# Up-projections of a two-layer transformer: seven products of quarters in place of eight, and modulation vectors moved between engines

## The chip, the cores and the metric

One core of one Trainium2 chip runs the whole program. The metric is the device time of one execution in microseconds (us). The kernel before takes 1658.03 us (median of three runs, 1656.92 to 1659.02).

The engines named here are PE (TensorE, matrix products; PEld is its loading of weights), DVE (VectorE), ACT (ScalarE), POOL (GpSimd) and SP (SyncE, which issues the loads of weights). Each works through its own queue in order.

## The reference, cut to what matters

512 latent tokens (x) and 256 context tokens (ctx), 1024 features, two layers. Layer 1 returns no context, so its feed-forward part runs for x alone.

```python
D_MODEL = 1024; SEQ = 512; CTX_LEN = 256; DEPTH = 2; D_FF = 2816

def swiglu(h, w_up, w_down):
    a, b = jnp.split(h @ w_up, 2, axis=-1)
    return (jax.nn.silu(a) * b) @ w_down

def layer(x, ctx, mod_x, mod_c, ...):
    sh1, sc1, gt1, sh2, sc2, gt2 = jnp.split(mod_x[:, None, :], N_MOD, axis=-1)
    csh1, csc1, cgt1, csh2, csc2, cgt2 = jnp.split(mod_c, N_MOD, axis=-1)
    hx = rmsnorm(x, g1) * (1 + sc1) + sh1
    hc = rmsnorm(ctx, g1) * (1 + csc1) + csh1
    ...                       # input projection, three kinds of mixers
    x = x + gt1 * (jnp.concatenate([conv_x, attn_x, gla_x], axis=-1) @ w_out)
    x = x + gt2 * swiglu(rmsnorm(x, g2) * (1 + sc2) + sh2, w_up, w_down)
    if ctx_out:               # layer 0 only
        ctx = ctx + cgt1 * (jnp.concatenate([conv_c, attn_c, gla_c], axis=-1) @ w_out)
        ctx = ctx + cgt2 * swiglu(rmsnorm(ctx, g2) * (1 + csc2) + csh2, w_up, w_down)
    return x, ctx

def reference(...):
    for l in range(DEPTH):
        mod_x = jax.nn.silu(c) @ w_mod[l] + b_mod[l]        # w_mod[l]: 1024 x 6144
        mod_c = jax.nn.silu(c_ctx) @ w_mod[l] + b_mod[l]
        x, ctx = layer(x, ctx, mod_x, mod_c, ...)
    return rmsnorm(x, final_norm_g)
```

## The kernel before

**Streams and products.** All streams are kept feature-major: 128 features on the partitions, the 768 tokens (512 in layer 1's second half) along the free side, eight chunks of features. Every dense product is made in three passes of a 32-bit format that the matrix engine takes at full rate (`float32r`): a value is split into a high part (a copy into that format, on ACT) and a low part (the difference, on DVE), and the passes are high by high, high by low, low by high. `dense_pass` (L707) runs them for one column block of 128 output features: for each run of tokens (`XS`, 512, and `CS`, 256) eight chunks times three matmuls into a PSUM bank of the pool `main` (three banks), and then it calls the given function that takes the bank out. A second pool of five banks, `bank`, serves everything else.

**Weights.** A list `plan` holds every block of weights in the order of use. `w_advance` (L500) issues their loads on SP's queue into a ring of four buffers `raw` (`RAWS`, 512 KB each); a buffer is given back once its reader is done. It splits each block at its arrival into `whi` (ACT) and `wlo` (DVE), two buffers of each.

**Order.** `Plan` keeps a rough clock for each engine while the program is written; chains of work (mixers, norms) are Python generators that are stepped in between the matmuls when that clock says that their inputs are there (`spawn`, `poll`, `until`). The order of the queues is thus fixed when the program is built.

**Feed-forward part** (L1618 on). The 22 blocks of 128 hidden features are taken in `F_BLOCKS` (L30): six, six, six and four. For each hidden block f there are two dense passes, `a` and `b`; the bank of `a` goes through Silu on ACT, that of `b` is multiplied by it on DVE, and the result is split into two parts. At the end of each block of blocks come eight down-projections whose results are added to the streams (`residual`). The hidden blocks 0 and 1 are made by `Firsts` (L725), which follows the norm chunk by chunk of its features, so that PE works while the norm (`Normed.task`, L894) is still being made. The norm takes per chunk and run of tokens two DVE operations (scale; low part) and one of ACT (shift; high part). The norm's sums come with the output projection before it: `tail` (L1594) ends x's tokens first (`o2` with seven blocks for x, then the same for ctx), so that x's norm starts while PE makes ctx's products. In layer 1 the two runs are the halves of x, 256 tokens each.

**Modulation vectors.** `mod_todo` (L356) lists the column groups of `w_mod` that come beside other work, 512 columns each. Groups 4 to 8 of layer 0 are made on PE (`mod_step`, L626, four steps for each group; a step has four matmuls and reads one `raw` buffer of 512 KB; after the fourth the sums are turned by four transposes), beside layer 0's mixers. Groups 9 to 11 of layer 0 and all twelve of layer 1 are made on DVE (`mod_step_v`, L660): per step two rows of weights, each scaled and added to two accumulators (x, ctx) of 128x512, and after the fourth step a transpose and a sum for each accumulator. `mod_items` (L359) places these steps in the list of weights: one after most items of the input projection, two after each `o1` block, and one after each up- or down-projection of layer 0.

## Time and profile before

| | |
|---|---|
| median of three runs | 1658.03 us |
| span of the profiled execution | 1655.9 us |
| matmul instructions on PE | 11021 |
| DVE, ACT, POOL instructions | 2016, 1194, 58 |
| weights of the up-projections, loads of 512 KB | 80 |
| loads of `w_mod` of 512 KB | 92 |

The span is what the profiler saw of one execution, from its first to its last instruction; that execution's own time as a run is not recorded, and the median of the runs lies 2.1 us above the span. A row of the profile's groups reads: line, engine, operation, output from inputs, shapes, number; then busy time and the mean of one; then the idle time before them and what ended it. A name such as `main` or `raw` is the pool's buffer. In a timeline, a row starts with its start and its length in us.

### The profile page before, as it was taken

Reading aid. Unit: us, or ns where it says so; the run is one execution under the profiler, and the core shown is the slowest. Engines: PE = TensorE matmul, PEld = TensorE weight load, DVE = VectorE, ACT = ScalarE, POOL = GpSimd, SP = SyncE. Lnnn points to the kernel's source line nnn. Section 1 sums busy time; section 2 is a strip of 40 time slices with the busy share of each in tenths; the row PEclk is TensorE's granted clock in tenths of the full one; section 3 lists DMA queues with packets and bytes.
Section 4 is the critical chain, followed back from the end, with each engine's and each line's share of the span. In section 5 each row is a group of like instructions: output and inputs, shape, how many; then the busy total and the mean of one; then the engine's idle time right before and its main releaser. Section 6 shows DMA issues by size and latency. Waiting matters only on the chain.

```text
span 1655.9 us, 26996 instructions
## 1 busy us (share of the span) xinstructions
PE 1619.7 (98%) x11021; PEld 1371.7 (83%) x11026; DVE 1056.2 (64%) x2016; ACT 598.7 (36%) x1194; POOL 35.7 (2%) x58
## 2 busy tenths in 40 slices
PE   7999999999999999999999999998999999999998
PEld 5878778888888888888888888786889888888887
DVE  5687877669867766767752366879787533333336
ACT  4454544543422122112212235555474422223224
POOL 2000000000000000000000000000000000000002
PEclk9999999999999999999999999999999999999999
DMA  9830312244234544444442152201123233232322
GB/s 259 253 100 15 90 52 77 83 160 138 67 115 124 145 125 121 138 128 140 127 118 71 33 146 52 64 27 52 65 77 90 77 89 106 83 117 84 100 85 77
DMA packets 252540, 168.45 MB, mean 102 GB/s; under 512 B 29700, under 2 KB 232960, under 8 KB 252416
## 3 DMA queue, kind: packets, MB, share of 16 engines
q1 hardware_dynamic: 248832, 155.93, 32.8%
q0 software_dynamic: 1760, 5.47, 1.1%
q10 hardware_dynamic: 1824, 5.31, 0.9%
q8 instruction: 87, 1.43, 0.4%
q14 instruction: 37, 0.30, 0.1%
HBM read 159.35 MB, written 7.34 MB: 101 GB/s over the span
## 4 chain that ended last, share of the span: by engine, by line
PE 83%; DVE 8%; ACT 2%; issue 1%; DMA 0%; SPq 0%; DVEq 0%; ACTq 0%
PE main L136 69%; PE bank L136 11%; DVE act L185 3%; PE bank L140 3%; DVE t L185 1%; DVE t L213 1%; ACT t L152 1%; DVE mx L204 1%; DVE wlo L185 1%; ACT t L174 0%; DVE t L190 0%; DMA raw<-in_w_mod_dram 0%; DVE t L196 0%; DVE t L1140 0%; DVE act L196 0%
## 5 line engine op out<-in xcount | busy, mean ns | idle before, releaser
L136 PE MATMUL main<-act,whi 128*128 128x512 f32 (+1 forms) x4160 | 1131.1, 357 | 1.3 <-ACT act L152 1.3
L136 PEld LDWEIGHTS main<-act,whi 128*128 128x128 f32 x4160 | 731.8, 189 | 115.2 <-issue 9.1
L136 PE MATMUL main<-act,wlo 128*128 128x512 f32 (+1 forms) x2080 | 735.8, 354 | 1.7 <-DVE wlo L185 1.7
L136 PEld LDWEIGHTS main<-act,wlo 128*128 128x128 f32 x2080 | 393.0, 189 | 57.5 <-issue 2.7
L174 ACT CAST whi<-raw 128x1024 fp32r<-128x1024 f32 (+3 forms) x194 | 189.9, 979 | 486.7 <-PE main L136 455.6
L185 DVE TENSOR_TENSOR wlo<-raw,whi 128x1024 fp32r<-128x1024 f32 (+3 forms) x194 | 219.4, 1131 | 181.7 <-ACT whi L174 178.9
L196 DVE SCALAR_TENSOR_TENSOR t<-raw,cst,t 128x512 f32<-128x512 f32 x210 | 148.3, 746 | 40.9 <-DMA raw<-in_w_mod_dram 40.5
L196 DVE SCALAR_TENSOR_TENSOR act<-main,mods,act 128x512 f32<-128x512 f32 (+1 forms) x160 | 97.8, 614 | 96.5 <-PE main L136 95.4
L185 DVE TENSOR_TENSOR t<-main,t 128x256 f32<-128x256 f32 (+1 forms) x73 | 43.9, 601 | 110.2 <-PE main L136 106.8
L174 ACT CAST act<-t 128x512 fp32r<-128x512 f32 (+3 forms) x102 | 61.0, 599 | 124.8 <-DVE t L185 124.3
L152 ACT ACTIVATE t<-bank,nm 128x256 f32<-128x256 f32 (+1 forms) x144 | 69.7, 496 | 60.2 <-DVE nm L196 55.5
L136 PE MATMUL main<-act 128*128 128x256 f32 (+1 forms) x576 | 88.6, 311 | 0.0
L136 PEld LDWEIGHTS main<-act 128*128 128x128 f32 x576 | 79.9, 191 | 6.1 <-issue 0.3
L185 DVE TENSOR_TENSOR act<-t,act 128x512 fp32r<-128x512 f32 (+5 forms) x110 | 73.6, 672 | 12.7 <-ACT act L174 10.5
L136 PE MATMUL bank<-act,whi 128*128 128x256 f32 (+3 forms) x336 | 74.9, 298 | 0.0
L152 ACT ACTIVATE t<-main 128x512 f32<-128x512 f32 x69 | 36.2, 525 | 88.9 <-PE main L136 88.7
L136 PE MATMUL bank<-act 64*64 64x64 f32 (+2 forms) x608 | 62.7, 273 | 3.6 <-DVE act L185 3.4
L185 DVE TENSOR_TENSOR act<-act 128x768 f32<-128x768 f32 (+7 forms) x84 | 64.7, 782 | 1.3 <-ACT t L174 1.1
L204 DVE TENSOR_REDUCE mx<-bank 128x2 f32<-128x512 f32 (+2 forms) x104 | 56.2, 561 | 14.2 <-PE bank L136 13.7
L140 PE MATMUL bank<-tab,t 128*128 128x128 f32 (+1 forms) x396 | 56.4, 277 | 4.1 <-DVE nm L196 1.7
L136 PE MATMUL bank<-t,t 128*64 128x128 f32 (+1 forms) x720 | 58.0, 283 | 1.7 <-DVE t L200 1.5
L136 PEld LDWEIGHTS bank<-act 64*64 64x64 f32 (+1 forms) x608 | 47.8, 161 | 12.9 <-issue 5.4
(133 smaller groups left out, 1208.7 us busy)
## 6 DMA issues: line engine op xcount, KB each, us to landing
raw<-in_w_mod_dram SPq DMA_DIRECT2D x92, 512.0 KB, 4.2
raw<-in_w_up_dram SPq DMA_DIRECT2D x80, 512.0 KB, 3.9
raw<-in_w_down_dram SPq DMA_DIRECT2D x48, 384.0 KB, 3.4
raw<-in_w_in_dram SPq DMA_DIRECT2D x26, 512.0 KB, 4.0
raw<-in_w_in_dram SPq DMA_DIRECT2D x16, 256.0 KB, 3.8
raw<-in_w_out_dram SPq DMA_DIRECT2D x16, 256.0 KB, 2.9
raw<-in_w_out_dram SPq DMA_DIRECT2D x32, 128.0 KB, 3.0
raw<-in_w_up_dram SPq DMA_DIRECT2D x16, 256.0 KB, 4.3
```

Source lines behind the costliest of these rows:

```text
L136: self.pin("pe", self.nc.tensor.matmul(out, lhsT, rhs, start=start, stop=stop, **kw))
L140: self.pin("pe", self.nc.tensor.transpose(out, in_, ident))
L152: ins = self.pin("act", self.nc.scalar.activation(out, in_, func, **kw))
L174: self.pin("act", self.nc.scalar.copy(out, in_))
L185: self.pin(eng, self._v(eng).tensor_tensor(out, a, b, op))
L196: self.pin(eng, self._v(eng).scalar_tensor_tensor(out, a, s, b, op0, op1))
L204: self.pin("dve", self.nc.vector.tensor_reduce(out, in_, AX.X, op))
L213: self.pin("dve", self.nc.vector.copy_predicated(out, mask, data))
```

## The change

**Products.** Write the weights of a hidden block f as four quarters: `a1` is the block's `a` column half and `a2` its `b` half, split by features into k < 512 and k >= 512: a11, a12 (512 features by 128 columns each, from the `a` half), a21, a22. The normed stream is split by tokens into two halves and by features into two: b11, b21 for the first half of tokens, and the second half enters only through differences. Seven products of (four feature chunks) x (half the tokens: 384 in layer 0, 256 in layer 1) in Winograd's form of the scheme replace eight. Every one has 4 x 3 matmuls, so a hidden block takes 84 matmuls of 384 (256) columns; before, it took 48 of 512 columns, and in layer 0 another 48 of 256.

**Operands.** `Quartered` makes the seven operands of the norm (b11, b21, t1, b22, t2, t3, t4), each with its own high and low part: the sums for t1 to t4 on DVE, the high parts on ACT, the low parts on DVE. `Unit.make` makes the seven operands of the weights (a11, a12, a22, s1, s2, s3, s4; 128x512 each): two sums on POOL, two on DVE, seven high copies on ACT, seven low subtractions on DVE. The two `raw` buffers of the unit are used in place for these sums, and are given back after their last use.

**Banks.** p1, p6, p7 and p4 add up in one bank of `main` per unit (`v`), which is read out after each; p2 and p5/p3 use banks of `bank`.

**Order.** `run_units` writes the products of neighbouring units alternately, and operands three products ahead (`AHEAD`). At the start of a layer's feed-forward part the first two units go product by product side by side, p1 and p2 first, as the norm's operands come; `Firsts` is no longer used for the up-projections. Layer 0 takes five blocks (5, 5, 4, 4, 4) in place of four.

**Modulation.** Groups 9 to 11 of layer 0 are made on PE too, all of them before `o2` (four steps after each `o1` block). Layer 1's steps are still on DVE; for groups 4 and up, whose ctx vector is used by nothing, only x's is made.

```diff
-F_BLOCKS = ((0, 6), (6, 12), (12, 18), (18, 22))
+F_BLOCKS = (((0, 5), (5, 10), (10, 14), (14, 18), (18, 22)), ((0, 6), (6, 12), (12, 18), (18, 22)))
...
-    mod_todo = [(0, g, half, kk) for g in range(4, 9) for half in range(2) for kk in range(2)]
-    mod_todo += [(l, g, q) for l in range(DEPTH) for g in range(0 if l else 9, 12) for q in range(4)]
+    mod_todo = [(0, g, half, kk) for g in range(4, 12) for half in range(2) for kk in range(2)]
+    mod_todo += [(1, g, q) for g in range(12) for q in range(4)]
...
-            if l == 0 and i >= 4:
+            if l == 0 and i >= 5:
                 mod_items(1)
         for j in range(4):
             out1_item(l, j)
             if l == 0:
-                mod_items(2)
+                mod_items(4)
...
+        ni = 1 if l == DEPTH - 1 and g >= 4 else 2
...
+    class Quartered(Normed):
+        WHERE = dict(b11=("a", 0), b21=("a", 1), t1=("b", 0), t3=("b", 1), t2=("c", 0), t4=("c", 1))
...
+        def split(self, name, kk, src):
+            hi, lo = self.at(name, kk)
+            S.acopy(hi, src)
+            S.tt(lo, src, hi.bitcast(F32), ALU.subtract)
+            self.have.add((name, kk))
...
+                S.stt(u, xT[k][:, t0:t1], A[:, 2 * k + s:2 * k + s + 1], pt[:, :t1 - t0], ALU.mult, ALU.mult)
...
+                S.act(h[:, t0:t1], u, AF.Identity, bias=mod(self.l, self.sh, k, s))
+                S.gave(ut)
+                if first:
+                    self.split("b21" if k >= 4 else "b11", kk, h[:, :w])
+                elif k < 4:
+                    S.tt(h[:, :w], h[:, :w], h[:, w:2 * w], ALU.subtract)
+                    self.split("t1", kk, h[:, :w])
+                else:
+                    self.split("b22", kk, h[:, w:2 * w])
...
+            for kk in range(4):
+                yield dict(act=self.new("t2", kk))
+                h, g = self.full[kk], self.full[kk + 4]
+                S.stt(h[:, :w], h[:, :w], -1.0, g[:, w:2 * w], ALU.mult, ALU.subtract)
+                self.split("t2", kk, h[:, :w])
...
+    SEVEN = dict(p1=("a11", "b11", "v", True), p2=("a12", "b21", "q", True), p3=("s4", "b22", "r", False),
+                 p4=("a22", "t4", "v", False), p5=("s1", "t1", "r", True), p6=("s2", "t2", "v", False),
+                 p7=("s3", "t3", "v", False))
...
+    class Unit:
...
+                S.tt(self.e[:, :512], R["a21"], R["a22"], ALU.add, eng="pool")
+                S.tt(R["a21"], R["a11"], R["a21"], ALU.add, eng="pool")
...
+            S.acopy(hi, src)
+            S.tt(lo, src, hi.bitcast(F32), ALU.subtract)
...
+            elif j in ("p3", "p6"):
+                if self.mid:
+                    S.tt(a2, pt, a2, ALU.add)
+                    S.act(a2, a2, AF.Silu)
+                else:
+                    S.acopy(a2, pt)
+                    self.mid = True
...
+            elif j == "p7":
+                S.tt(self.tb[:, :w], pt, self.tb[:, :w], ALU.add)
+            elif j == "p4":
+                S.stt(a1, pt, -1.0, a1, ALU.mult, ALU.mult)
+                S.gave(self.banks["v"])
+                S.stt(a2, self.tb[:, :w], -1.0, a2, ALU.mult, ALU.mult)
...
+    AHEAD = 3
...
+        if start:
+            for j in ("p1", "p2", "p5", "p3", "p6", "p7"):
+                seq += [(0, j), (1, j)]
+            seq += [(0, "p4"), (2, "p1"), (1, "p4"), (2, "p5"), (2, "p2")]
+            u = 2
+        else:
+            seq += [(0, "p1"), (0, "p5"), (0, "p2")]
+            u = 0
+        while u < n - 1:
+            seq += [(u, "p3"), (u, "p6"), (u + 1, "p1"), (u, "p7"), (u + 1, "p5"), (u, "p4"), (u + 1, "p2")]
+            u += 1
...
-                Firsts((l, "up"), (ga, gb)).run(norm, lambda i, s, pt: evs[i % 2]("ab"[i // 2], s, pt))
...
-                for nm in ("a", "b"):
-                    dense_pass([(nm, *w_next((l, nm, f)), 0)], X, sg, ev_ab)
-                    mod_steps()
...
+            for f in range(f0, f1):
+                units.append(Unit(l, f, norm, f == f1 - 1))
+            run_units(units, bi == 0)
```

Three places in the queues are shown, each before and then after the change. A row has the line, the operation, output from inputs (pool names with a number for each buffer) and the shape; `x3` stands for three in a row.

DVE at the start of layer 0's feed-forward part, before: the norm's scale (`act, A, bank`) and low part (`act<-t3, mods0, act`), the sums of squares (`t3<-t3,t3`), ends of the output projection (`act<-main, mods0, act`) and modulation steps (`raw, cst`).

```order
L196 SCALAR_TENSOR_TENSOR t3_4841<-act_3935,A_4838,bank_4802 128x512
L185 TENSOR_TENSOR t3_4591<-t3_4591,t3_4855 128x256
L196 SCALAR_TENSOR_TENSOR act_3939<-main_4858,mods0_136,act_3939 128x256
L196 SCALAR_TENSOR_TENSOR t3_4540<-raw_5056,cst_144,t3_4540 128x512
L196 SCALAR_TENSOR_TENSOR act_4840<-t3_4841,mods0_136,act_4840 128x512
L185 TENSOR_TENSOR t3_4591<-t3_4591,t3_4872 128x256
L196 SCALAR_TENSOR_TENSOR t3_4880<-act_3935,A_4838,bank_4802 128x512
L196 SCALAR_TENSOR_TENSOR act_3941<-main_4875,mods0_136,act_3941 128x256
L196 SCALAR_TENSOR_TENSOR act_3941<-main_4897,mods0_136,act_3941 128x256
L196 SCALAR_TENSOR_TENSOR act_4879<-t3_4880,mods0_136,act_4879 128x512
```

The same place after: 384-wide rows are the norm's sums (`t3<-t3`) and low parts (`act<-t3, act`), `whi`/`wlo` rows of 512 are the weights' low parts (the tile's name is that of the buffer that holds both parts).

```order
L199 SCALAR_TENSOR_TENSOR t3_5062<-act_3867,A_4881,bank_4968 128x256
L188 TENSOR_TENSOR whi_5055<-t3_5004,whi_5055 128x512
L199 SCALAR_TENSOR_TENSOR t3_5070<-act_3871,A_4881,bank_4845 128x512
L188 TENSOR_TENSOR t3_4927<-t3_4927 128x384
L199 SCALAR_TENSOR_TENSOR t3_5078<-act_3869,A_4881,bank_4968 128x256
L199 SCALAR_TENSOR_TENSOR t3_5086<-act_3873,A_4881,bank_4845 128x512
L188 TENSOR_TENSOR act_5066<-t3_4927,act_5066 128x384
L188 TENSOR_TENSOR act_4931<-t3_5069,act_4931 128x384
L188 TENSOR_TENSOR t3_4961<-t3_4961 128x384
L199 SCALAR_TENSOR_TENSOR t3_5094<-act_3869,A_4881,bank_4968 128x256
L188 TENSOR_TENSOR act_4965<-t3_5085,act_4965 128x384
L188 TENSOR_TENSOR act_5082<-t3_4961,act_5082 128x384
```

What moved: the modulation steps are gone from here; a chunk of the norm now has the differences and one more low part behind its scale, and the operands of the first two units' weights stand among them.

PE at the end of the last `o1` block and the start of `o2` in layer 0, before (`act, whi` and `act, wlo` are the passes of a dense product):

```order
L136 MATMUL main_4521<-act_3707,whi_4304 128x256 x2
L136 MATMUL main_4521<-act_3707,wlo_4305 128x256
L136 MATMUL main_4521<-act_3878,whi_4304 128x256 x2
L136 MATMUL main_4521<-act_3878,wlo_4305 128x256
L136 MATMUL main_4558<-act_1230,whi_4465 128x512 x2
L136 MATMUL main_4558<-act_1230,wlo_4466 128x512
```

After, with the last four steps of modulation (`raw, cst`) and their transposes in between:

```order
L139 MATMUL main_4560<-act_3622,wlo_4487 128x256
L139 MATMUL main_4560<-act_3748,whi_4486 128x256 x2
L139 MATMUL main_4560<-act_3748,wlo_4487 128x256
L139 MATMUL bank_4574<-raw_4494,cst_144 32x256 x3
L139 MATMUL bank_4574<-raw_4500,cst_144 32x256 x4
L139 MATMUL bank_4574<-raw_4508,cst_144 32x256 x4
L139 MATMUL bank_4574<-raw_4510,cst_144 32x256 x4
L143 MATMUL bank_4574<-tab_82,t3_4604 128x128 x4
L139 MATMUL main_4615<-act_1224,whi_4582 128x512 x2
L139 MATMUL main_4637<-act_1224,whi_4582 128x256 x2
```

What moved: four blocks of `w_mod` are now read from the ring of `raw` buffers between the last weights of `o1` and the first of `o2`.

PE in layer 1's up-projections, before: the end of one product of 512 columns and the start of the next, in another bank.

```order
L136 MATMUL main_13838<-act_13065,whi_13802 128x512 x2
L136 MATMUL main_13838<-act_13065,wlo_13803 128x512
L136 MATMUL main_13838<-act_13092,whi_13802 128x512 x2
L136 MATMUL main_13838<-act_13092,wlo_13803 128x512
L136 MATMUL main_13874<-act_12861,whi_13834 128x512 x2
L136 MATMUL main_13874<-act_12861,wlo_13835 128x512
```

After, in the middle of two units: the last three chunks of p1 of the next unit, p7 of this one (bank `main_13839`), p5 of the next, and the first chunk of p4 of this one, into the same bank as p7.

```order
L139 MATMUL main_13976<-act_13156,whi_13922 128x256 x3
L139 MATMUL main_13976<-act_13193,whi_13922 128x256 x3
L139 MATMUL main_13976<-act_13213,whi_13922 128x256 x3
L139 MATMUL main_13839<-act_13222,wlo_13940 128x256 x3
L139 MATMUL main_13839<-act_13294,wlo_13940 128x256 x3
L139 MATMUL main_13839<-act_13310,wlo_13940 128x256 x3
L139 MATMUL main_13839<-act_13326,wlo_13940 128x256 x3
L139 MATMUL bank_14012<-act_13222,whi_13956 128x256 x3
L139 MATMUL bank_14012<-act_13294,whi_13956 128x256 x3
L139 MATMUL bank_14012<-act_13310,whi_13956 128x256 x3
L139 MATMUL bank_14012<-act_13326,whi_13956 128x256 x3
L139 MATMUL main_13839<-act_13456,wlo_13973 128x256 x2
```

What moved: a bank of `main` no longer holds one finished product, but is added to four times, with a read by DVE or ACT in between and one other product ahead of the next addition.

More of the change, by code (lines that the diff above doesn't have):

```diff
@@ L124, in op, with mm @@
         self.on = engine
-    def mm(self, out, lhsT, rhs, start, stop, tile_position=None):
+    def mm(self, out, lhsT, rhs, start, stop, tile_position=None, more=False):
         n = free_size(rhs)
@@ L660, in mod_step_v @@
     def mod_step_v(l, g, q):
+        ni = 1 if l == DEPTH - 1 and g >= 4 else 2
         if q == 0:
-            S.room(t3=2)
-            mod_now["acc"] = [tmp(), tmp()]
+            S.room(t3=ni)
+            mod_now["acc"] = [tmp() for _ in range(ni)]
         acc = mod_now["acc"]
@@ new lines, in product_t, with run_units @@
+    def product_t():
+        if S.fits(dict(act=1)):
+            t = act_t(F32R)
+            return (t[:, 0], t[:, 1]), [t]
+        S.room(t3=2)
+        ts = [tmp(dt=F32R) for _ in range(2)]
+        return tuple(ts), ts
+    AHEAD = 3
+    def run_units(units, start):
+        n = len(units)
+        seq = []
+        if start:
[3 more added lines that the diff above has]
+            u = 2
+        else:
+            seq += [(0, "p1"), (0, "p5"), (0, "p2")]
[3 more added lines that the diff above has]
+            u += 1
+        seq.pop()
+        seq += [(u, "p6"), (u, "p3"), (u, "p7"), (u, "p2"), (u, "p4")]
+        made = 0
+        for i, (u, j) in enumerate(seq):
+            while made < min(len(seq), i + AHEAD + 1):
+                v, jj = seq[made]
+                units[v].make(SEVEN[jj][0])
+                made += 1
+            units[u].run(j)
+        mod_steps()
@@ L1658, in hybrid_kernel @@
         S.preload()
-        keys = [(l, "d", len(F_BLOCKS) - 1, m) for m in range(NK)]
+        keys = [(l, "d", len(blocks) - 1, m) for m in range(NK)]
         if not last:
```

252 lines of the change are left out of this document (194 added, 58 removed).

## The prediction

> **What bounds the kernel now.** First the page: the busy times, the slices of PE and of its clock, and the chain of work that ended last.
>
> ```profile
> span 1655.9 us, 26996 instructions
> PE 1619.7 (98%) x11021; PEld 1371.7 (83%) x11026; DVE 1056.2 (64%) x2016; ACT 598.7 (36%) x1194; POOL 35.7 (2%) x58
> ...
> PE   7999999999999999999999999998999999999998
> ...
> PEclk9999999999999999999999999999999999999999
> ...
> PE 83%; DVE 8%; ACT 2%; issue 1%; DMA 0%; SPq 0%; DVEq 0%; ACTq 0%
> ```
>
> PE is busy 98% of the span at full clock, so fewer matmuls would shorten it, as long as nothing else comes late. How much the others have to spare differs by stage, which the table of windows shows (length, then busy time of PE, PEld, DVE, ACT, POOL, then the clock):
>
> ```profile
> 420.00:440.00 20.00, 20.00 (x125) 17.77 (x124) 18.31 (x43) 9.63 (x19) 0.00 (x0) 1.00 0.18 53
> 540.00:873.00 333.00, 333.00 (x1991) 292.41 (x1989) 226.40 (x357) 64.58 (x93) 0.00 (x0) 1.00 0.45 130
> 1275.00:1290.00 15.00, 13.89 (x114) 13.22 (x113) 10.95 (x32) 7.72 (x17) 0.00 (x0) 1.00 0.00 1
> 1305.50:1640.00 334.50, 334.50 (x1551) 280.06 (x1549) 130.87 (x167) 95.17 (x128) 6.09 (x6) 1.00 0.31 92
> ```
>
> The second and fourth rows are the feed-forward parts of the layers: PE never pauses, DVE is busy 68% and 39%. The first row is the start of layer 0's: no pause either, but DVE is at 92%. The third, the start of layer 1's, loses 1.1 us. So PE's saving counts in full in the long stretches, while DVE has little room at the two starts. I go by stage.
>
> **Products: about -66 us.** Two pieces of PE's timeline, for 512 and for 256 columns:
>
> ```profile
> 606.97 0.61 PE L136 MATMUL main<-act,whi 128*128 128x512 f32 x2
> ...
> 607.65 0.61 PE L136 MATMUL main<-act,whi 128*128 128x512 f32 x2
> 603.06 0.40 PE L136 MATMUL main<-act,whi 128*128 128x256 f32 x2
> ...
> 603.42 0.40 PE L136 MATMUL main<-act,whi 128*128 128x256 f32 x2
> ```
>
> Three matmuls take 0.68 us, so 0.227 each; of 256 columns 0.36, 0.120 each. 384 columns do not occur in a dense product; between these rows I take the middle, 0.173 (ends 0.120 and 0.227; linear in the columns, as these two nearly are). Layer 0: before 1056 x (0.227 + 0.120) = 366 us, after 22 x 84 = 1848 x 0.173 = 320: -46. Layer 1: before 1056 x 0.227 = 239 and 1.3 more for the halves in `Firsts`, after 1848 x 0.120 = 222: -19. The products of zeros that `Firsts` opens and closes go too, some 1.5 us.
>
> **Modulation on PE: +8, and +5 of waits.** A step on PE, four transposes and the jump to the next work:
>
> ```profile
> 348.33 0.64 PE L136 MATMUL bank<-raw,cst 128*32 128x256 f32 x8
> 348.90 1.09 PE L136 MATMUL bank<-act 128*128 128x256 f32 x6
> 422.61 0.60 PE L140 MATMUL bank<-tab,rst 128*128 128x128 f32 x4
> 422.97 3.83 PE L136 MATMUL main<-act 128*128 128x256 f32 x30
> 426.64 0.60 PE L136 MATMUL bank<-zero 128*128 128x512 bf16 x2
> 426.89 0.58 PE L136 MATMUL main<-act,whi 128*128 128x512 f32 x1
> raw<-in_w_out_dram SPq DMA_DIRECT2D x16, 256.0 KB, 2.9
> ```
>
> A step is 0.57 us, four transposes 0.36: 12 x 0.57 + 3 x 0.36 = 7.9 us on a PE that had no pause. The steps also read the ring of four buffers. Where four stand in a row behind an `o1` block, the next block's load waits on SP for the first of them to be read, then takes 2.9 us, and its split about 1.2: 5 us, of which the other steps and transposes cover about 2. I count two such places less what attention still has to do there: +5 (nothing to 12, at four bare places).
>
> **The start of the feed-forward parts: +30.** DVE's timeline at layer 0's start before, a pair for 512-wide subtractions, and the first scale and the end of `o2` in layer 1:
>
> ```profile
> 422.66 0.74 DVE L196 SCALAR_TENSOR_TENSOR t<-raw,cst,t 128x512 f32<-128x512 f32 x1
> 423.32 0.74 DVE L196 SCALAR_TENSOR_TENSOR t<-act,A,bank 128x512 f32<-128x512 f32 x1
> 423.98 0.42 DVE L185 TENSOR_TENSOR t<-t,t 128x256 f32<-128x256 f32 x1
> 424.31 0.48 DVE L196 SCALAR_TENSOR_TENSOR act<-main,mods,act 128x256 f32<-128x256 f32 x1
> 424.71 0.74 DVE L196 SCALAR_TENSOR_TENSOR t<-raw,cst,t 128x512 f32<-128x512 f32 x1
> ...
> 1628.19 0.69 DVE L185 TENSOR_TENSOR act<-raw,act 128x512 fp32r<-128x512 f32 x1
> 1628.79 0.62 DVE L185 TENSOR_TENSOR t<-t,t 128x256 f32<-128x256 f32 x1
> 1273.40 0.47 DVE L196 SCALAR_TENSOR_TENSOR t<-act,A,bank 128x256 f32<-128x256 f32 x1
> 1277.97 0.39 PE L136 MATMUL main<-zero 128*128 128x512 bf16 x1
> ```
>
> In a row, from start to start, a scalar-tensor-tensor takes 0.66 (512) and 0.40 (256), a tensor-tensor 0.60 and 0.33; for 384 I take the middles, 0.53 and 0.47. After the change DVE has, in its queue from the first scale to the last low part of t4, in layer 0: 8 and 12 scalar-tensor-tensor of 512 and 256, 9 of 384; tensor-tensor 16 of 512, 42 of 384, 4 of 256: 5.3 + 4.8 + 4.8 + 9.6 + 19.7 + 1.3 and 0.5 of small ones = 46 us. The first scale stood at 423.3, so they end at 469 at the soonest. The norm's small chain, the high parts awaited from ACT, the evictions awaited from PE and two sums of POOL (below) add some 5, which gives 474, and the last chunk of p4 takes about 1. PE is free at 426.9 and by then has the first two units and two products of the third to make, 16 x 12 x 0.173 = 33 us, to 460. So PE waits about 15 us. Layer 1: 17 tensor-tensor of 512, 46 of 256 and 29 scalar-tensor-tensor of 256, 10.2 + 15.2 + 11.6 + 0.5 = 37.5 from 1273.4: 1311, with the same 5, 1316; PE from 1278.0 with 16 x 1.44 = 23: 1301. 15 us, less the 1.1 that were lost before. Together +30; without the waits +20, and with stretched ones +45. Behind t4 DVE still owes the first outputs and the third unit's operands: +3. The order on PE can't cover this: all operands of the norm pass through DVE, and the weights' too.
>
> **The long stretches: +11.** Per unit DVE makes seven low parts and two sums of 512 (9 x 0.60 = 5.4), three additions and two multiplications (0.33 and 0.40 in layer 1; 0.47 and 0.53 in layer 0) and a low part of the product (0.60; 0.86 for 768): 7.8 us in layer 1 against PE's 84 x 0.120 = 10.1, and 8.7 against 14.6 in layer 0. There the modulation steps come on top. From the groups (line, engine, operation, shapes, number, then busy us and mean ns), with the loads' time to landing last:
>
> ```profile
> L196 DVE SCALAR_TENSOR_TENSOR t<-raw,cst,t 128x512 f32<-128x512 f32 x210 | 148.3, 746 | 40.9 <-DMA raw<-in_w_mod_dram 40.5
> L209 DVE STREAM_TRANSPOSE t<-t 128x512 f32<-128x512 f32 x30 | 19.7, 690 | 0.0
> L204 DVE TENSOR_REDUCE part<-t 128x16 f32<-128x512 f32 x30 | 18.9, 664 | 0.0
> L190 POOL TENSOR_SCALAR act<-act,vec 128x256 f32<-128x256 f32 x8 | 9.6, 1196 | 432.2 <-ACT t L152 432.0
> L200 POOL COPY act<-t 64x512 f32<-64x512 f32 x4 | 3.1, 784 | 188.2 <-DVE t L213 188.1
> L174 ACT CAST act<-raw 128x512 fp32r<-128x512 f32 x24 | 14.6, 621 | 15.6 <-DMA raw<-in_w_out_dram 11.6 <-DMA raw<-in_w_down_dram 3.0 <-PE bank L136 0.9
> raw<-in_w_up_dram SPq DMA_DIRECT2D x80, 512.0 KB, 3.9
> ```
>
> An accumulator costs about 8 x 0.66 + 0.60 + 0.58 = 6.4 us over four steps, 1.6 a step, 3.2 with two. The change nearly halves them (30 accumulators to 16); that is DVE's time beside a busy PE and is worth nothing by itself. A unit of layer 0 thus has at most 11.9 us of DVE. ACT's copies and Silus of a unit, thirteen of 0.62 at most, are 8.1 us and stay beside PE. POOL's sums, two a unit of 128x512 with two inputs, have no row: the nearest are 0.78 (a copy of 512) and 2.4 (two scalings of 256); I take 1.2, nearer to the copy, which moves the same count of elements, with half as much again for the second input. The Trainium skill's page "GPSIMD Engine Reference" (section 3.1) gives 4.5 us for an addition of 2048 elements; by that a sum here is an estimated 1.1 us, and the total would not move. No run here shows it.
>
> What POOL does to DVE is seen where they ran at once, first two copies on POOL and an addition on DVE beside them (with the mean of its kind), then two scalings on POOL:
>
> ```profile
> 131.60 2.40 POOL L200 COPY act<-t 64x768 f32<-64x768 f32 x2 [61.68 <-DVE es L185]
> 133.19 0.83 DVE L185 TENSOR_TENSOR es<-es,den 128x2 f32<-128x2 f32 x1
> L185 DVE TENSOR_TENSOR es<-es,den 128x2 f32<-128x2 f32 x72 | 11.9, 165 | 17.4 <-ACT es L152 16.5
> 1627.91 2.58 POOL L190 TENSOR_SCALAR act<-act,vec 128x256 f32<-128x256 f32 x2 [421.67 <-ACT t L152]
> ```
>
> A tiny addition that takes 0.165 on average took 0.83 and ended with POOL's copy; but the 512-wide subtraction at 1628.19, in the middle of POOL's scaling, took its normal 0.60. So a POOL operation holds DVE for part of its time: I take 0.85 for each, 1.7 a unit. That puts DVE at 9.5 of 10.1 in layer 1 and up to 13.6 of 14.6 in layer 0. Since p6, p7 and p4 add into one bank with a read in between and one product (1.4 or 2.1 us) ahead of the next, some of DVE's jams reach PE: +6 in layer 1 (0 to 15). In layer 0 a loop of the ring comes near the unit's time as well: last read of a buffer, 3.9 us of load, 2.4 of POOL's sums, then the operands three products ahead: 13 to 15.6 us against 14.6: +5 (0 to 12). The fifth block of layer 0 costs DVE 8 x (0.66 + 0.40) us of additions, hidden by PE, and one more turn between blocks: +2 (0 to 5).
>
> **Sum**, against the profiled span: -66.5 + 8 + 5 + 30 + 3 + 11 + 2 = -7.5, 1648.4; the median stood 2.1 above the span, so **1650**. All low ends (nothing for the 3 either) give 1619, all high ends 1691.
>
> **Rivals.** *DVE keeps up* (1627): the starts cost 20, rings and jams nothing, o1's waits 2. For it: DVE at 39% in layer 1 before; against it: the count of 46 us, which has few rows to shrink. Chance 0.24.
>
> *POOL's sums hold DVE* (1725, slower): each sum takes 2.4 us and DVE stands for all of it. Then DVE needs 7.8 + 4.8 = 12.6 a unit in layer 1, 2.5 over PE for 20 units, and 16.7 at worst in layer 0, 2 over PE for the 8 units with two accumulators, and the ring's loop gets 2 longer for some 10 others: +50 +16 +20 in place of 11. It decides from a hold of 1.15 us per sum in layer 1. For it speaks 133.19, against it 1628.19. The Trainium skill, "SBUF — State Buffer", section "Who interferes with whom", says that a DVE instruction with two SBUF inputs and a GpSimd instruction that reads SBUF share a port pair, and that whoever comes second stands fully still. The row at 133.19 agrees (0.83 in place of 0.165), the one at 1628.19 does not (0.60). Chance 0.15.
>
> *DVE's queue is late at the shared bank* (1675, slower): the read of p6 or p7 has 1.44 us in layer 1; with 0.2 to start and 0.33 for itself, it misses when more than 0.9 us stands ahead of it, two subtractions. Twice a unit 0.6 late over 20 units of layer 1, and 0.3 in layer 0: +36 in place of 11. For it: DVE's queue is fixed and mixes 512-wide work with these reads; against it: a stall of PE gives DVE time to catch up. Chance 0.15.
>
> *384 columns cost as much as 512* (+99, 1749): against it stand the 256-column rows at nearly half. Chance 0.02.
>
> **How the numbers follow.** My forecast (1636 to 1664) gets 0.44. The range, 1619 to 1700, leaves out the second and fourth rivals, 0.17 together, and reaches to the third's price with the high ends of the starts and of o1's waits on top (15 + 7): 1697. A measurement can tell 0.2% here, 3.3 us. Below 1654.7: 0.24 and two thirds of 0.44, together 0.53. Within 0.2%: a quarter of the forecast's and a little of the third rival, 0.13. Above: 0.34.
>
> **What would show it.** Right: in a table of windows PE loses some 15 us in the 50 us behind the end of each `o2`, with DVE near full there; units of 14.6 and 10.1 us on PE behind that; POOL's sums near 1.2. Wrong: a POOL row of 2 us or more with DVE subtractions of twice 0.69 beside it; idle time of PE ended by DVE's `t<-main` rows all along layer 1; matmuls of 384 columns off 0.173; no idle time at the starts.

## The result, and the profile after

The changed kernel takes 1673.49 us (median of four runs, 1671.38 to 1675.58) against 1658.53 before (1656.92 to 1659.88): ratio 1.009, 95% interval 1.0076 to 1.0105. It is slower by 15 us; the prediction was 1650 and faster. The time lies inside the stated range, on the other side of no change.

The page of the changed kernel: its span, its busy times, and the slices of PE and of PE's clock.

```profile
span 1673.8 us, 29358 instructions
PE 1594.3 (95%) x11530; PEld 1403.7 (84%) x11530; DVE 1246.5 (74%) x2399; ACT 757.1 (45%) x1611; POOL 168.0 (10%) x146
...
PE   7999999998899999999999999999998899999998
...
PEclk9999999999999999999999999999998999999999
```

PE has 25 us less to do and 79 us of pauses where it had 36; DVE has 190 us more, POOL 132 us more. Two dents stand in PE's row, at slices 10 to 11 and 31 to 32: ahead of and at the starts of the two feed-forward parts; the clock dips at the second. A few rows of PE's timeline, before and then after, mark the stages: layer 1's first product (two products of zeros open it), the first up-projection of layer 0 (128x384), layer 1's first product again, and the first up-projection of layer 1.

```profile
985.94 0.60 PE L136 MATMUL bank<-zero 128*128 128x512 bf16 x2
```

```profile
444.58 0.34 PE L139 MATMUL main<-act,wlo 128*128 128x384 f32 x1
...
985.80 0.60 PE L139 MATMUL bank<-zero 128*128 128x512 bf16 x2
...
1276.88 0.67 PE L139 MATMUL main<-act,wlo 128*128 128x256 f32 x4
```

With the same marks in the runs below this table follows (us of PE's timeline between the marks; "up to" is the end of the last `o2` product, some 0.2 from the first up-projection):

| kernel | up to layer 0's feed-forward | layer 0's feed-forward | layer 1's mixers | layer 1's feed-forward, to the end |
|---|---|---|---|---|
| before | 426.8 | 559.1 | 292.2 | 377.8 |
| after | 444.7 | 541.1 | 291.2 | 396.8 |
| modulation alone (e1) | 441.5 | 558.3 | 292.3 | 377.4 |
| without POOL's sums (e4) | 443.3 | 526.2 | 291.3 | 374.7 |
| POOL's sums unused (e5) | 444.3 | 540.2 | 292.5 | 396.0 |
| sums on DVE (e6) | 445.4 | 532.7 | 291.6 | 382.9 |
| without the norm's low parts (e10) | 443.4 | 531.5 | 292.3 | 387.0 |
| modulation alone, some at o2 (e13) | 435.5 | 558.1 | 290.2 | 377.4 |
| seven products in layer 0 only, sums on DVE, some at o2 (e15) | 435.6 | 530.7 | 291.6 | 377.1 |

The change loses 18 us ahead of layer 0's feed-forward part, gains 18 in it and loses 19 in layer 1's. Each row is one profiled execution. The windows of after, in which PE is watched from each start to the last low part of t4 (rows 1 and 3), and behind it:

```profile
444.58:494.00 49.42, 39.95 (x188) 34.89 (x187) 45.62 (x93) 33.93 (x70) 6.25 (x5) 0.90 0.16 43
540.00:860.00 320.00, 313.99 (x1845) 294.86 (x1845) 253.07 (x402) 110.05 (x194) 37.95 (x26) 1.00 0.42 125
...
1276.88:1320.60 43.72, 33.00 (x193) 30.49 (x191) 38.20 (x91) 27.58 (x69) 5.76 (x4) 0.77 0.17 48
1320.60:1640.00 319.40, 305.04 (x2108) 283.22 (x2107) 220.04 (x350) 145.96 (x284) 59.22 (x38) 1.00 0.32 93
```

In these rows the length comes first, then the busy time of PE, PEld, DVE, ACT and POOL, then the granted clock. At the starts PE stands for 9.5 and 10.7 us beside a DVE that is 92% and 87% busy, at a clock of 0.90 and 0.77. Behind them, where before the change it never paused, it loses 6.0 and 14.4 us, and there DVE is only 79% and 69% busy. So DVE's share does not explain the long stretches; one of their pauses shows a way (rows of POOL, DVE and PE in layer 1):

```profile
1410.68 1.28 POOL L188 TENSOR_TENSOR t<-raw 128x512 f32<-128x512 f32 x1 [11.86 <-DMA raw<-in_w_up_dram]
1412.05 1.63 POOL L188 TENSOR_TENSOR raw<-raw 128x512 f32<-128x512 f32 x1
...
1410.83 1.69 DVE L188 TENSOR_TENSOR whi<-raw,whi 128x512 fp32r<-128x512 f32 x1
...
1412.78 1.45 DVE L188 TENSOR_TENSOR wlo<-raw,wlo 128x512 fp32r<-128x512 f32 x1
...
1417.55 0.42 DVE L188 TENSOR_TENSOR t<-main,t 128x256 f32<-128x256 f32 x1
...
1415.17 1.60 PE L139 MATMUL main<-act,wlo 128*128 128x256 f32 x12
1418.12 1.67 PE L139 MATMUL main<-act,whi 128*128 128x256 f32 x12 [1.35 <-DVE t L188]
```

Two of DVE's subtractions, 0.69 us each elsewhere, take 1.69 and 1.45 us beside POOL's two sums. DVE is 1.8 us late after them and catches up row by row; but the row at 1417.55 takes p6 or p7 out of the shared bank, and PE stands 1.35 us for it.

The rows also show for how long DVE is held. At 1410.83 POOL's sum has 1.13 us left, and the subtraction takes 1.00 more than its 0.69; at 1412.78 it has 0.90 left, and the subtraction takes 0.76 more. Both stand until some 0.14 us before the sum's end. So do all 56 two-input additions and subtractions of DVE that read SBUF alone and start beside one of POOL's sums in this trace, within 0.06 us; the 37 DVE operations with an input in PSUM that start there are not longer. It works the other way too: the sum at 1412.05 starts when the subtraction before it has 0.47 us left, and takes 1.63 in place of 1.28.

### The profile page after: what moved, and what is told of

Its sections match the earlier page's. It is cut to its first block, busy times and chain, and to the rows that moved or that the text cites. A ratio compares the mean times of both kernels' runs of the same rounds, so it can differ in the third digit from the quotient of the medians.

```text
span 1673.8 us, 29358 instructions
## 1 busy us (share of the span) xinstructions
PE 1594.3 (95%) x11530; PEld 1403.7 (84%) x11530; DVE 1246.5 (74%) x2399; ACT 757.1 (45%) x1611; POOL 168.0 (10%) x146
## 5 line engine op out<-in xcount | busy, mean ns | idle before, releaser
L139 PE MATMUL main<-act,whi 128*128 128x512 f32 (+2 forms) x2656 | 623.6, 342 | 19.9 <-DVE t L188 11.8
L139 PEld LDWEIGHTS main<-act,whi 128*128 128x128 f32 x2656 | 440.3, 190 | 70.2 <-ACT whi L177 18.5
L139 PE MATMUL main<-act,wlo 128*128 128x256 f32 (+2 forms) x1856 | 463.2, 332 | 12.4 <-DVE t L188 7.4
L177 ACT CAST whi<-raw 128x512 fp32r<-128x512 f32 (+4 forms) x238 | 175.2, 739 | 279.2 <-PE main L139 214.4
L139 PE MATMUL bank<-act,wlo 128*128 128x256 f32 (+2 forms) x872 | 163.7, 318 | 15.6 <-ACT act L177 14.5
L199 DVE SCALAR_TENSOR_TENSOR act<-main,mods,act 128x256 f32<-128x256 f32 (+1 forms) x176 | 107.6, 614 | 80.6 <-PE main L139 79.0
L139 PEld LDWEIGHTS bank<-act,wlo 128*128 128x128 f32 (+1 forms) x872 | 139.8, 196 | 21.4 <-ACT act L177 17.5
L139 PEld LDWEIGHTS bank<-act,whi 128*128 128x128 f32 (+1 forms) x952 | 150.6, 193 | 5.7 <-ACT whi L177 1.8
L139 PE MATMUL main<-t,whi 128*128 128x512 f32 (+1 forms) x560 | 151.6, 354 | 0.0
L188 DVE TENSOR_TENSOR wlo<-raw,whi 128x1024 fp32r<-128x1024 f32 (+4 forms) x114 | 113.0, 991 | 34.1 <-ACT whi L177 33.3
```

What stands on the lines that cost most here:

```text
L139: self.pin("pe", self.nc.tensor.matmul(out, lhsT, rhs, start=start, stop=stop, **kw))
L177: self.pin("act", self.nc.scalar.copy(out, in_))
L188: self.pin(eng, self._v(eng).tensor_tensor(out, a, b, op))
L199: self.pin(eng, self._v(eng).scalar_tensor_tensor(out, a, s, b, op0, op1))
```

## The experiments

Ratios are against the kernel before, measured beside each group of runs (1658.6 to 1659.3 us).

**e1: the modulation part alone**, on the kernel before.

```diff
-    mod_todo = [(0, g, half, kk) for g in range(4, 9) for half in range(2) for kk in range(2)]
+    mod_todo = [(0, g, half, kk) for g in range(4, 12) for half in range(2) for kk in range(2)]
...
-                mod_items(2)
+                mod_items(4)
```

> The kernel before with the modulation part of the change alone (groups 9 to 11 of layer 0 on PE, four steps behind each o1 block; ctx vectors that nothing reads dropped). Theory A, from the two traces: the first up-projection starts 17.9 us later after the change (444.6 against 426.6), of which 8 us are PE's own work and the rest waits for the ring's loads plus the half-speed clock that the pauses bring; all of it comes with this part, so about 1676 us. Rival B: only the 8 us of work belong to this part and the rest to the way the output projection and the new norm meet: about 1667 us. Rival C: DVE freed beside the feed-forward part gives something back: 1660 us or less.

1671.97 us, ratio 1.0076 (1.0056 to 1.0096): 13 us, all of them ahead of the feed-forward part (441.5 against 426.8 in the profiles). Between A and B; the part as a whole costs what the prediction's two terms, 8 and 5, gave it. Hardly anything comes back in the feed-forward part (558.3 against 559.1).

**e2 and e3: the seven products in one layer only**; the other layer is written as before.

```diff
-        norm = Quartered(l, V_N2, 4, 3, n)
+        norm = Quartered(l, V_N2, 4, 3, n) if l in SEVENL else Normed(l, V_N2, 4, 3)
```

> The changed kernel with the seven products in layer 0 alone; layer 1's up-projections are made as before. Theory A (each layer's part adds up by itself: +17.9 ahead of layer 0's feed-forward part, -18.1 in it, +18.7 in layer 1's): about 1658 us, as before the change. Rival B (what slows layer 1 is the state in which layer 0 leaves the chip, such as the modulation steps or the ring): over 1668 us.

> The changed kernel with the seven products in layer 1 alone; layer 0's up-projections are made as before, with the changed modulation steps beside them. Theory A (the parts add up): 1658.5 + 17.9 + 18.7, about 1695 us. Rival B (layer 0's part is the loss and layer 1's pauses are hidden elsewhere): 1676 us or less.

1654.19 us (0.9969, 0.9957 to 0.9981) and 1694.33 us (1.0211, 1.0187 to 1.0234). The parts add up, within 4 us of theory A in both runs: against e1, layer 0's products win 18 us and layer 1's lose 22; the modulation loses 13.

**e4 and e5: POOL's sums left out, and POOL's work put back without its results being awaited.**

```diff
-                S.tt(self.e[:, :512], R["a21"], R["a22"], ALU.add, eng="pool")
-                S.tt(R["a21"], R["a11"], R["a21"], ALU.add, eng="pool")
...
-                src = self.e[:, :512]
+                src = R["a22"]
```

and for e5, on top of that:

```diff
+                S.tt(self.e[:, :512], R["a21"], R["a22"], ALU.add, eng="pool")
+                S.tt(self.e[:, :512], R["a22"], R["a21"], ALU.add, eng="pool")
```

> The changed kernel without the two sums of weights that POOL makes for each hidden block (they are left out: the operands that need them take an addend in their place). Theory A (DVE is late at the shared bank mostly because POOL's operations hold it): the 88 sums of 1.5 us hold DVE for some 0.8 us each, the 13 us of pauses behind layer 1's start and the 9 behind layer 0's fall by more than half, about 1660 us. Rival B (DVE's own queue is late, POOL matters little): pauses in the long stretches as after the change, 1670 us or more.

> As the run without POOL's sums, but POOL makes two additions of 128x512 for each hidden block that nobody waits for (their result is not used; the operands still take an addend in place of the sums). It tells apart what the 36 us between 1673 and 1637 are. Theory A (POOL's operations hold DVE while both read two streams): most of the 36 come back, 1665 us or more. Rival B (the operands s1 to s4 come late because they wait for POOL's results, and the ring of loads with them): it stays near 1637 us, 1645 at most.

Both kernels leave the sums out of what s1 to s4 are made of; DVE and PE have as many instructions as in the change. 1637.07 us (0.9863, 0.9842 to 0.9883) without POOL's work, 23 us below A's figure, and 1674.39 us (1.0095, 1.008 to 1.011) with as many sums on POOL that no operand waits for. All 37 us come back, so what POOL's operations do to the others while they run can cost all of it, without a wait for their results. The groups show to whom; POOL's sums and DVE's low parts of the weights in e5:

```profile
L188 POOL TENSOR_TENSOR t<-raw 128x512 f32<-128x512 f32 x88 | 134.2, 1527 | 879.9 <-DMA raw<-in_w_up_dram 472.5 <-ACT t L155 181.3 <-DVE act L199 55.3
L188 DVE TENSOR_TENSOR whi<-raw,whi 128x512 fp32r<-128x512 f32 x153 | 117.7, 770 | 36.3 <-ACT whi L177 34.6
L188 DVE TENSOR_TENSOR wlo<-raw,wlo 128x512 fp32r<-128x512 f32 x146 | 112.3, 770 | 25.4 <-ACT wlo L177 23.2
```

and the same DVE groups in e4:

```profile
L188 DVE TENSOR_TENSOR whi<-raw,whi 128x512 fp32r<-128x512 f32 x153 | 105.1, 688 | 39.2 <-ACT whi L177 36.9
L188 DVE TENSOR_TENSOR wlo<-raw,wlo 128x512 fp32r<-128x512 f32 x146 | 100.4, 688 | 36.1 <-ACT wlo L177 34.2
```

One and the same list of DVE instructions takes 1263.6 us in e5 and 1212.1 in e4: 52 us for 88 operations of POOL, 0.6 us each on average, with single instructions held for 0.7 to 1.1 us in layer 1's long stretch (22 of them beside 39 operations of POOL; none in e4).

It does not follow that the changed kernel loses its 36 us by held instructions alone. DVE's list takes 1246.5 us there, 34 more than in e4 and not 52. It also waits for POOL's results, which e5 does but once, for 2.6 us. The list of waits of the changed kernel (us in total, times, longest):

```profile
DVE raw L188 <- POOL raw L188: 19.2, 11, 2.6
ACT whi L177 <- POOL t L188: 13.0, 8, 4.4
ACT wlo L177 <- POOL t L188: 2.2, 4, 1.0
```

That the change and e5 agree within 1 us is therefore in part chance, and how the 36 us divide between holds and waits in layer 0, where all but 4.4 us of these waits lie, stays open. In layer 1's long stretch the holds stand nearly alone: PE's pauses that end with DVE's read of the shared bank are 9.6 us in the change, 9.8 in e5 and none in e4.

**e6: the two sums on DVE** (`eng="pool"` dropped in both lines).

> The changed kernel with the two sums of a hidden block on DVE in place of POOL. DVE gets 1.2 us more for each hidden block (9.0 of 10.1 us in layer 1), POOL nothing. Theory A (holds): 1673 - 36 + about 6 for DVE's higher load, 1643 us. Rival B (DVE's load decides): 1673 us or more, with longer pauses ended by DVE in layer 1.

1652.78 us (0.9968, 0.9957 to 0.998). 20.7 us below the changed kernel although DVE has 1.2 us more of its own work for each hidden block: the sums cost more on POOL, with the holds and the waits that they bring, than on DVE itself. It is 10 us above A's figure, though, so DVE's load matters as well (layer 1's part 382.9 against 374.7 in e4). DVE is as long busy as in e5, and the kernel is 21.6 us faster (e5's page, then e6's):

```profile
PE 1593.3 (95%) x11530; PEld 1402.7 (84%) x11530; DVE 1263.6 (76%) x2399; ACT 758.0 (45%) x1611; POOL 170.2 (10%) x146
PE 1585.2 (96%) x11530; PEld 1399.3 (85%) x11530; DVE 1260.6 (76%) x2487; ACT 760.6 (46%) x1611; POOL 35.9 (2%) x58
```

So DVE's total alone does not decide: holds of up to 1.1 us at a time, wherever POOL's sums happen to run, cost more than as much work in the order of DVE's own queue.

**e7: products of zeros in PE's pauses at the starts.**

```diff
+                    for _ in range(FILL.get((self.l, j, kk), 0)):
+                        S.mm(dummy[0], zero[:, :P], zero, True, True)
```

> The changed kernel with 44 products of zeros on PE (512 columns) put before the chunks of p1, p2 and p3 of each layer's first hidden block, where PE waits for the norm. Theory A (the pauses at the starts bring half-speed stretches, 10 us of them at layer 0's start and 20 at layer 1's, which cost half their length): the stretches shrink to 7 us in all, the zeros themselves fall into the pauses but for a few us: 1673 - 12 + 5, about 1666 us. Rival B (the clock halves for another reason): the stretches stay, and the zeros add 3 to 10 us: 1676 us or more.

The zeros also hold one of the three banks of `main` during the start. 1680.73 us (1.0138, 1.0123 to 1.0153). The windows of the two starts:

```profile
443.00:495.00 52.00, 45.15 (x224) 36.50 (x224) 47.02 (x92) 33.90 (x70) 5.71 (x4) 0.93 0.15 41
1280.70:1325.20 44.50, 37.27 (x235) 30.02 (x235) 39.32 (x91) 27.90 (x69) 5.44 (x4) 0.92 0.17 48
```

The granted clock rises from 0.77 to 0.92 at layer 1's start and from 0.90 to 0.93 at layer 0's, so the half speed does come from the pauses; but the stretch from the start to the last low part of t4 does not get shorter (44.5 us against 43.7). A higher clock that is bought with zeros gains nothing there, where PE waits for DVE. What the half speed alone costs, e7 does not tell, since the zeros and the bank that they hold cost time of their own. A's clock was right and its gain wrong.

**e8: more room at the shared bank.**

```diff
-            seq += [(u, "p3"), (u, "p6"), (u + 1, "p1"), (u, "p7"), (u + 1, "p5"), (u, "p4"), (u + 1, "p2")]
+            seq += [(u, "p3"), (u, "p6"), (u + 1, "p1"), (u + 1, "p5"), (u, "p7"), (u + 1, "p2"), (u, "p4")]
...
-        seq.pop()
+        seq.remove((u, "p2"))
```

> The changed kernel with p5 of the next hidden block moved ahead of p7 and p2 of the next ahead of p4, so that two other products stand between p6 and p7 in the shared bank, and one between p7 and p4. Theory A (DVE's read of p6 or of p7 comes late): pauses ended by DVE's row out of PSUM in the long stretches (13 us in layer 1, 9 in layer 0) fall by half, about 1663 us. Rival B (DVE falls behind for long spells, so that one product more of room changes nothing): 1670 us or more, the same pauses elsewhere.

1678.19 us (1.0124, 1.0099 to 1.0148). In layer 1's long stretch the pauses that DVE's read of the bank ends fall from 9.6 us to 0.9, but those that wait for the weights' operands rise from 4.7 to 10.1, and the time does not fall. Held instructions are not why the operands are late: DVE's list takes 1232.3 us, 14 less than in the change. DVE and ACT wait for POOL's results instead, 52 and 53 us in the whole kernel in place of 19 and 15:

```profile
DVE raw L188 <- POOL raw L188: 52.2, 18, 4.4
ACT whi L177 <- POOL t L188: 30.4, 12, 3.8
ACT wlo L177 <- POOL t L188: 22.9, 10, 3.5
```

So the room at the bank was exchanged for later sums, and e8 does not tell whether a held DVE would do no harm with that room.

**e9 and e13: the modulation part alone, its steps placed otherwise**: spread over the input projection, or (e13) two behind each `o1` block and one behind each `o2` block. The edits are shown against e1.

```diff
             if l == 0 and i >= 5:
-                mod_items(1)
+                mod_items(2 if i % 4 else 1)
...
-                mod_items(4)
+                mod_items(1)
```

```diff
-                mod_items(4)
+                mod_items(2)
...
             out2_item(l, m, m >= N_OUT2)
+            if l == 0:
+                mod_items(1)
```

> The kernel before with the modulation part alone, as in the first experiment (1672.0), but its steps on PE spread over the input projection (two behind most of its blocks, one behind each o1 block), so that four never stand in a row. Theory A (of the 13 to 15 us of that part 8 are PE's work and the rest waits of o1 and o2 for the ring): 1667 us. Rival B (the steps cost the same wherever they stand): 1672 us.

> The kernel before with the modulation part alone, its steps on PE placed as in the first experiment beside the input projection, but two behind each o1 block and one behind each o2 block (groups 10 and 11, which only the end of the feed-forward part reads). Theory A (beyond 8 us of PE work the part costs what o1 and o2 wait for the ring of loads when four steps stand in a row, 1672.0 in the first experiment): 1667 us. Rival B (PE's work for a step is dearer than its 0.57 us, wherever it stands): 1671 us or more.

1682.47 us (1.0141, 1.0126 to 1.0156), above both of e9's figures, and 1664.01 us (1.0031, 1.0019 to 1.0043), below A's. Windows of e1, e9 and e13, to the end of `o2`, and of e9 among the mixers:

```profile
360.00:441.50 81.50, 74.67 (x536) 61.00 (x533) 45.21 (x96) 27.49 (x61) 0.00 (x0) 0.98 0.41 130
```

```profile
200.00:300.00 100.00, 86.44 (x823) 68.13 (x824) 67.94 (x172) 40.83 (x116) 2.23 (x2) 0.86 0.19 59
...
360.00:400.00 40.00, 40.00 (x318) 32.09 (x317) 28.09 (x77) 20.28 (x60) 0.00 (x0) 1.00 0.32 112
400.00:440.00 40.00, 40.00 (x228) 33.30 (x227) 22.91 (x36) 12.50 (x21) 0.00 (x0) 1.00 0.40 122
```

```profile
360.00:435.45 75.45, 74.42 (x545) 58.27 (x541) 44.05 (x98) 26.60 (x61) 0.00 (x0) 1.00 0.47 147
```

With four steps in a row PE stands 6.8 us around `o1` and `o2`; with at most two it stands 1.0. Spread over the mixers, the steps open 13.6 us of pauses there instead (86.4 of 100 us, where the kernel before has 97.1 in its own profile); why the mixers' order bears them so badly was not tried. At `o2` the whole part costs 4.7 us (8.7 ahead of the feed-forward part, of which the later stages give some back).

**e10: the norm's low parts left out.**

```diff
             S.acopy(hi, src)
-            S.tt(lo, src, hi.bitcast(F32), ALU.subtract)
             self.have.add((name, kk))
...
-                for i, (a, x) in enumerate(((hi, xh), (hi, xl), (lo, xh))):
+                for i, (a, x) in enumerate(((hi, xh), (hi, xh), (lo, xh))):
```

> The changed kernel without the norm's low parts in the up-projections (the 28 subtractions of each layer are left out; the products that would read a low part read the high one). DVE loses 28 x 0.47 = 13 us at layer 0's start and 28 x 0.33 = 9 us at layer 1's, PE's work is the same. Theory A (DVE's queue from the first scale to the last low part sets the start: 54 and 48 us measured): both starts get shorter by nearly that, 1673 - 20, about 1653 us. Rival B (PE's half speed or the high parts on ACT set the start): 1668 us or more.

1657.52 us (0.9992, 0.9983 to 1.0002), 16 us below the change and 4.5 above A's figure. PE's work is the same; with 13 and 9 us less on DVE layer 0's part is 9.6 us shorter and layer 1's 9.8. DVE's queue sets both starts, as predicted.

**e11, e12, e14, e15: versions put together from this.**

> The seven products in both layers, the sums of weights on DVE, the modulation steps spread over the input projection: 1652.8 (sums on DVE) less 5 for the spread steps, about 1648 us. If the spread steps gain nothing: 1653.

> The seven products in layer 0 alone, the sums of weights on DVE, the modulation steps spread. Layer 0's part took 532.7 us with the sums on DVE against 541.2, layer 1's 382.9 against 377.8 as before the change: 1654.2 - 8.5 - 5, about 1641 us. If the gains do not add up: 1646 or more.

> The seven products in layer 0 alone, the sums of weights on DVE, the modulation steps where the change puts them: 1654.2 (layer 0 alone) less 8.5 for the sums, 1646 us. If POOL's hold matters only in layer 1: 1654.

> As e14, with the modulation steps placed as in e13: 1646 less 5, 1641 us. If the steps cost the same wherever they stand: 1646.

1657.97 us (1.0001, 0.9989 to 1.0013) and 1654.63 us (0.9974, 0.9963 to 0.9985) with the spread steps, both above what was expected: against the same products with the steps where the change has them (e6 and e14) the spreading costs 5.2 and 6.8 us; in e9 it cost 10.5 against e1. With the steps where the change has them, e14: 1647.88 us (0.9935, 0.9915 to 0.9955). With some of them at `o2`, e15: 1638.93 us (0.9883, 0.9866 to 0.9899), 20 us faster than before and 35 faster than the change. Its page:

```profile
span 1635.0 us, 27147 instructions
## 1 busy us (share of the span) xinstructions
PE 1590.2 (97%) x10837; PEld 1371.0 (84%) x10842; DVE 1128.2 (69%) x2173; ACT 683.6 (42%) x1385; POOL 35.6 (2%) x58
```

## Why the prediction was wrong, step by step

- **Products, -66 us: right.** Twelve matmuls of 384 columns start every 2.08 us, 0.173 each:

```profile
823.83 2.24 PE L139 MATMUL main<-act,wlo 128*128 128x384 f32 x12
825.91 2.24 PE L139 MATMUL main<-act,whi 128*128 128x384 f32 x12
```

- **Modulation, +8 and +5: right** (13 us alone, e1), the waits being at the four steps in a row (e13). That the steps would not be hidden by anything was right too: 8.7 us ahead of the feed-forward part in e13, where PE hardly waits. In the changed kernel's profile this stage is 17.9 us longer, 3.2 more than in e1; the cause of these 3.2 was not looked for.
- **The starts, +30 and +3: right in kind.** DVE needs from the first scale to the last low part of t4 54.0 us in layer 0 and 48.2 in layer 1, where the prediction had 51 and 42.5; without POOL's sums it is 49.5 and 39.3 (e4). In the two windows of the starts PE makes 180 matmuls of 384 columns and 187 of 256, at 0.173 and 0.120 worth 31 and 22 us, in 49.4 and 43.7: 18 and 21 us are lost. The half-speed clock that the pauses bring was not in the sum; e7 shows no gain from lifting it with zeros.
- **The long stretches, +11: here the prediction failed.** The step is the price of POOL's sums: "a POOL operation holds DVE for part of its time: I take 0.85 for each, 1.7 a unit", and then "some of DVE's jams reach PE: +6 in layer 1", with +5 for a loop of the ring in layer 0. Measured, the sums cost 36 us (the change against e4), starts included: 14.9 in layer 0's feed-forward part and 22.1 in layer 1's by the profiles. The hold was not taken too small. A sum takes 1.5 us, not 1.2, and a two-input operation of DVE that starts beside it stands for nearly all that is left of it, but not every sum meets one: over 88 sums DVE's list is 34 us longer, 0.4 each, half of what was taken. What it makes of the time was mis-sized: DVE's load per unit stays below PE's, as calculated, and so it was treated as spare time with a few jams. In fact most of it came back as time of the kernel: 52 us of holds cost 37 in e5, 0.85 for each of 44 hidden blocks. The pause shown above suggests why, a lump of 1.8 us on a queue with deadlines one product (1.44 us) apart; that the other pauses come about in the same way is argued, not shown. The prediction's own sign of it came: in layer 1's long stretch PE is idle eight times until a `t<-main` row of DVE.
- **The other terms** hold, in part by errors that cancel. The two feed-forward parts together are 1.0 us longer after the change, though their products save 66.5: 67.5 us are lost there, and the sum had 46 (30, 3, 11 and 2). In e4 it is 30.5, and the sum without its +11 has 35.
- The ring's loop in layer 0 was not measured by itself. In the change DVE waits 15.7 us there for POOL's results and ACT 14.5, and POOL in its turn waits for weights to land; but e5, without these waits and with more holds, takes as long in that part (540.2 against 541.1).
- **The rivals.** "POOL's sums hold DVE" was the right mechanism, at two thirds of its time per sum (1.5 in place of 2.4) and for DVE's operations with two inputs in SBUF only; its point of decision (a hold of 1.15 us per sum, where DVE's load passes PE's) was the wrong criterion: it hurt below that. "DVE's queue is late at the shared bank" named the place at which it shows in layer 1, and its price (1675) came nearest, but DVE's own queue is not the cause: without POOL's sums no pause of layer 1's long stretch ends there (e4), and with the sums on DVE 0.6 us do (e6). Both were given 0.15.
- What was weighed wrongly: the row at 1628.19, a subtraction that ran freely in the middle of a scaling on POOL, was taken to show that POOL holds DVE for only part of its time. It can be read the other way: the addition before it on DVE was running when the scaling began, and the two scalings took 2.58 us where single ones take 1.16 to 1.20 each, so POOL may have been the one that stood; no run tells. Of the Trainium skill's page "SBUF — State Buffer", section "Who interferes with whom", the exclusive port agrees with e5: DVE's subtractions have two SBUF inputs, and they are longer beside POOL's sums (0.770 on average against 0.688), while DVE's additions with one input in PSUM kept their 0.419 (128x256) with and without them.

## What to carry to other kernels

A busy share below one says that an engine has room on average, not that a hold of 1 to 2 us in its queue is free: compare the longest lump with the distance between the reads that others wait for. Before work is given to an idle engine, ask what that engine shares with the one it relieves, and who will wait for its results: here the same additions cost 21 us less on the busy engine than on the idle one. And where a saving on the bottleneck moves work to a second engine, look stage by stage at which of them sets the pace (layer 0, with 384 columns of PE's work for each operand of the weights, gained; layer 1, with 256, did not).

## What the runs showed of the hardware that was not expected

- A sum of 128x512 on POOL takes 1.28 to 1.97 us in the change, 1.5 on average. A subtraction of that size on DVE (0.69) that starts beside one stands until some 0.14 us before the sum's end, in e5 for up to 1.13 us. A sum that starts beside such a subtraction stands in its turn; two of the 74 DVE operations that start beside a sum in e5 were not held (at 504.80 and 517.81), and there the sums took 1.90 and 2.09 us.
- PE's half-speed stretches after pauses are multiples of 3.41 us in the trace's record of the clock (13.65 and 6.83 us at layer 1's start), and products of zeros in the pauses prevent most of them there (6.83 us are left in e7). That made the kernel no faster while PE waited for another engine.
